# Far queries copied into contiguous tiles by GpSimd, in the attention of a hybrid decoder layer

## The chip, the core and the metric

One core of a Trainium2 chip runs the whole program. Its engines run side by side, each through its own instructions in order: TensorE (PE: matmuls; PEld: the loads of the weights that a matmul holds still while its other operand streams), VectorE (DVE), ScalarE (ACT), GpSimd (POOL) and SyncE (SP), which here only issues DMAs. The metric is the device time of one execution in microseconds, as a median over runs. The profile is of one execution more.

## What is computed

One decoder layer over 2048 positions of width 1024, in float32: an input projection; eight heads of dilated attention beside pooling groups; an output projection; a gated MLP; an embedding gate; a last norm. The change concerns the attention. Cut from the reference:

```python
DIL_PATTERNS = ((128, 1), (512, 4), (2048, 16))
...
    s = jnp.einsum('bnqrhd,bnkrhd->bnrhqk', qb, kk)      # query blocks against [previous, current] keys
    s = s - slopes[:, None, None] * dist                 # ALiBi
    s = jnp.where(valid[:, None, None], s, -jnp.inf)
    m = jnp.max(s, axis=-1, keepdims=True)
    e = jnp.exp(s - m)
    den = jnp.sum(e, axis=-1)
    o = jnp.einsum('bnrhqk,bnkrhd->bnqrhd', e, vv) / den_t[..., None]
...
    w = d * jnp.exp(m - jnp.max(m, axis=0, keepdims=True))
    w = w / jnp.sum(w, axis=0, keepdims=True)
    return jnp.sum(w[..., None] * o, axis=0)             # branches weighted by their denominators
```

Dilation d joins positions of the same residue modulo d. The kernel treats dilation 1 as the near branch and dilations 4 and 16 together as the far branch, by residues modulo 4.

## The kernel before

Attention (`phase_attention`) runs after the input projection and before the output projection and the rest. It has 128 steps: eight heads with sixteen blocks of 128 queries. For the near branch the block is 128 neighbouring positions; for the far branch it is 128 positions of one residue r modulo 4 (every fourth position), against 128, 256, 384 or 512 keys of that residue. Four steps make up a head's residue; it begins with the step of 512 keys, by the order `CFG["perm"]`, and the others have 256, 384 and 128.

A head's queries lie in two tiles, `qhh` and `qll` (high and low parts of the float32 numbers, 128 x 2048), the keys in `ks`, biases in `nb` and `fb`. SP loads them a head ahead. In a step TensorE forms the near scores `sn` (L573, L574: weights are slices of `qhh` and `qll`, keys stream) and the far scores `sf` (L562, L563); VectorE adds the bias and finds the extreme (L578, L584); ScalarE takes the exponential (L590, L594); TensorE transposes (`tp`, L604); ScalarE and VectorE split the result (`pth`, L617; `ptl`, L621); TensorE multiplies by the values (`o`, L632, L646). Before, the far queries were read with a step of four elements:

```python
            t.qr = t.qhh.rearrange("p (c r) -> p r c", r=4)
```

Once a residue, a result `o` of the far and one of the near branch is copied to a staging tile `ev` (by ScalarE and VectorE, L670). Half of it has to change partitions: SP sends it by a DMA (`s<-ev`, L671) into `s1` (near) or `s3` (far), and three steps later GpSimd adds the other half (L672). After each pair of heads the statistics are turned, stored to DRAM (`std`, `stf`) and read back in another layout (`sn`, `sf` of L809, not the scores), and weights `wd` are stored. Later, while the next pair runs, the two branches of the finished pair are mixed in four chunks of 512 positions: SP fetches weights `wb` (L913), GpSimd multiplies `s1` and `s3` by them and adds (`m1`, `m3`, L940, L942, L949), and SP stores the sum to `mr` (L952). For the third pair the chunks come every four steps, for the others every seven. The fourth pair is mixed by VectorE at the start of the output projection, whose weights are `wo` (raw: `rwo`, L985).

The instructions of PE, ACT, DVE and POOL stand in the order in which this code issues them: in each step the stages of `CFG["ord"]`, with their lags. Stage F is the far scores, G the sums on GpSimd, M the mixing. SP's DMAs are placed by the framework. A tile with several buffers can be written again when its last reader is done; a wait for that stands on the engine or queue that writes it.

Of the kernel before, what the change touches and what calls it, by code (L numbers as in the profile page):

```python
# [10 lines left out]
F32 = mybir.dt.float32  # L11
F32R = mybir.dt.float32r
AF = mybir.ActivationFunctionType
ALU = mybir.AluOpType
# [3 lines left out]
P = 128  # L18
# [8 lines left out]
CH = 512  # L27
NCH = S // CH
NQ = S // P
# [21 lines left out]
def fp(ap):  # L51
    return ap.bitcast(F32)


def rdma(nc, dst, src):
    nc.sync.dma_start(fp(dst) if dst.dtype == F32R else dst, fp(src) if src.dtype == F32R else src)
# [429 lines left out]
def phase_attention(tc, g, mx, near_b, far_b):  # L486
# [3 lines left out]
    nc = tc.nc  # L490
    NS = H * NQ
    LAST = 4 * H - 2
    with ExitStack() as ctx:
        sb = ctx.enter_context(tc.tile_pool(name="b_sb", bufs=1, reuse_waits="tile"))
# [5 lines left out]
        heads, steps, groups, pairs = {}, {}, {}, {}  # L500

        def load_qk(h):
            t = heads[h] = Shared()
            pr, e = h // 2, h % 2
            rows = slice(DH * e, DH * e + DH)
            t.qhh = sb.tile([P, S], F32R, tag=f"qhh{e}", bufs=1, name=f"qhh{h}")
            t.qll = sb.tile([P, S], F32R, tag=f"qll{e}", bufs=1, name=f"qll{h}")
            t.qr = t.qhh.rearrange("p (c r) -> p r c", r=4)
            t.qlr = t.qll.rearrange("p (c r) -> p r c", r=4)
            t.ks = sb.tile([P, NCH, 4, P], F32R, tag=f"ks{e}", bufs=1, name=f"ks{h}")  # L510
            t.nb = sb.tile([P, 256], F32, tag=f"nb{e}", bufs=1, name=f"nb{h}")
            t.fb = sb.tile([P, 512], F32, tag=f"fb{e}", bufs=1, name=f"fb{h}")
            twice = lambda z: z[pr][rows, None].to_broadcast([DH, 2, S])
            return [
                (t.qhh, twice(g.qh)),
                (t.ks.rearrange("p c r j -> p (c r j)"), g.kk[pr][rows].rearrange("d a c r j -> d a (c r j)")),
                (t.qll, twice(g.ql)),
                (t.fb, far_b[h]),
                (t.nb, near_b[h]),
            ]  # L520
# [5 lines left out]
        def load_v(pr, which, q):  # L526

            v = sb.tile([P, 4, 2, P], F32R, tag=which, bufs=4, name=f"{which}_{pr}_{q}")
            vals[pr, which, q] = v
            src = near_v[:, 4 * q : 4 * q + 4, pr, :] if which == "v1" else far_v[q, :, :, pr, :]  # L530
            return v.rearrange("p b h d -> p b (h d)"), src
# [24 lines left out]
        def far_scores(s):  # L556
            st = steps[s]
            t = st.t
            st.fv = ps_f.tile([P, CH], F32, tag="f", name="sf")[:, : st.wf]
            keys = t.ks[:, : st.nf, st.r, :]  # L560
            cl = slice(st.i * P, (st.i + 1) * P)
            nc.tensor.matmul(st.fv, t.qr[:, st.r, cl], keys, start=True, stop=False)  # L562
            nc.tensor.matmul(st.fv, t.qlr[:, st.r, cl], keys, start=False, stop=True)  # L563

        def near_scores(s):
            st = steps[s]
# [91 lines left out]
        def halves(pt, gi, near):  # L658
            h, q = divmod(gi, 4)
            e = h % 2  # L660
            mine = slice(DH * e, DH * e + DH)
            other = slice(DH * (1 - e), DH * (1 - e) + DH)
            return e, mine, other, pt.s1[:, q * CH : (q + 1) * CH] if near else pt.s3[:, q, :]

        def copy_out(copy, gi, near):

            e, mine, other, dst = halves(pairs[gi // 8], gi, near)
            o = groups[gi].o[near]
            t = sb.tile([P, CH], F32, tag="ev", bufs=8, name="ev")
            copy(t, o)  # L670
            nc.sync.dma_start(dst[mine], t[other])  # L671
            sums.later(3, lambda: nc.gpsimd.tensor_tensor(dst[mine], dst[mine], t[mine], op=ALU.add))  # L672

        def add_out(gi, near):
            e, mine, other, dst = halves(pairs[gi // 8], gi, near)
            o = groups[gi].o[near]
            ev = sb.tile([P, CH], F32, tag="ev", bufs=8, name="ev")
            nc.scalar.copy(ev[mine], o[other])
            nc.vector.tensor_tensor(dst[mine], o[mine], ev[mine], op=ALU.add)

# [20 lines left out]
        def fold(v):  # L701
            gi, part = v // 4, v % 4
            if part == 1 and gi < LAST:
                copy_out(nc.scalar.copy, gi, False)
# [44 lines left out]
        with tc.manual_schedule(engines=set(EN.values())):  # L749
            for dst, src in load_qk(0):  # L750
                rdma(nc, dst, src)
            for q in range(4):
                for which in ("v3", "v1"):
                    rdma(nc, *load_v(0, which, q))
            queue = []
            stages = {
                "F": far_scores, "N": near_scores, "fm": far_max, "nm": near_max, "fe": far_exp, "ne": near_exp,
                "T": turn, "h": high, "l": low, "V": values, "W": values_b, "S": stats, "M": mix, "o": fold, "p": folded, "B": begin, "G": shifts
            }
            for s in range(NS + 10):  # L760
                if s < NS:
                    h, n = divmod(s, NQ)
                    if n == 1 and h + 1 < H:
                        queue += load_qk(h + 1)
                    if queue and n % 2:
                        rdma(nc, *queue.pop(0))
                    for pr in range(1, NPAIR):
                        if s - 2 * NQ * (pr - 1) in V_STEPS:
                            rdma(nc, *load_v(pr, *V_STEPS[s - 2 * NQ * (pr - 1)]))
                if s == NS + 2:  # L770
                    last_far(nc, g, mx, ps_t, pairs[NPAIR - 1])
                    pieces = pairs[NPAIR - 1].pieces = last_weights(nc, mx, pairs[NPAIR - 1])
                for nm, lag in CFG["ord"]:
                    if 0 <= s - lag < NS or nm in "MG":
                        stages[nm](s - lag)
                for _ in range({NS + 3: 3, NS + 4: 2, NS + 5: 1}.get(s, 0)):
                    next(pieces)
# [63 lines left out]
def last_weights(nc, sb, pt):  # L841

    both = (pt.near, pt.far)
    lo = sb.tile([P, CH], F32, tag="m1", bufs=2, name="lo")[:8]
    nc.vector.tensor_tensor(lo, pt.near[0], pt.far[0], op=ALU.min)
    yield
    for mx_, _ in both:
        nc.vector.tensor_tensor(mx_, lo, mx_, op=ALU.subtract)
    yield
    for ex, _ in both:  # L850
        nc.scalar.activation(ex, ex, AF.Exp)
    yield
    for ex, dn in both:
        nc.vector.tensor_tensor(dn, ex, dn, op=ALU.mult)
    yield
    nc.vector.tensor_tensor(lo, pt.near[1], pt.far[1], op=ALU.add)
    yield
    nc.vector.reciprocal(lo, lo)
    yield
    pt.w = []  # L860
    for ex, _ in both:
        hi, low = (sb.tile([P, CH], F32R, tag=f"wb{y}", bufs=2, name=f"w{y}")[:8] for y in range(2))
        nc.vector.tensor_tensor(ex, ex, lo, op=ALU.mult)
        nc.scalar.copy(hi, ex)
        nc.vector.tensor_tensor(low, ex, fp(hi), op=ALU.subtract)
        pt.w.append((hi, low))
    yield
# [47 lines left out]
    pt.__dict__.setdefault("wb", {})[c] = wb  # L915


def mix_products(nc, g, sb, eng, pt, c):
    cs = slice(c * CH, (c + 1) * CH)
    wb = pt.wb.pop(c)  # L920
    m1 = sb.tile([P, CH], F32, tag="m1", bufs=2, name="m1")
    m3 = sb.tile([P, CH], F32, tag="m3", bufs=1, name="m3")
    eng.tensor_tensor(m1, pt.s1[:, cs], wb[0], op=ALU.mult)
    eng.tensor_tensor(
        m3.rearrange("p (i r) -> p i r", r=4),
        pt.s3.rearrange("p r i -> p i r")[:, c * P : c * P + P, :],
        wb[1].rearrange("p (i r) -> p i r", r=4),
        op=ALU.mult,
    )
    eng.tensor_tensor(m1, m1, m3, op=ALU.add)  # L930
    pt.m1 = m1


def mix_steps(nc, g, sb, pr, pt, c):

    cs = slice(c * CH, (c + 1) * CH)
    wb = pt.wb.pop(c)
    m1 = sb.tile([P, CH], F32, tag="m1", bufs=2, name="m1")
    m3 = sb.tile([P, CH], F32, tag="m3", bufs=1, name="m3")
    nc.gpsimd.tensor_tensor(m1, pt.s1[:, cs], wb[0], op=ALU.mult)  # L940
    yield
    nc.gpsimd.tensor_tensor(  # L942
        m3.rearrange("p (i r) -> p i r", r=4),
        pt.s3.rearrange("p r i -> p i r")[:, c * P : c * P + P, :],
        wb[1].rearrange("p (i r) -> p i r", r=4),
        op=ALU.mult,
    )
    yield
    nc.gpsimd.tensor_tensor(m1, m1, m3, op=ALU.add)  # L949
    yield  # L950
    yield
    nc.sync.dma_start(g.mr[pr][:, cs], m1)  # L952
    yield


# [1054 lines left out]
```

## Time and profile before

| | us |
|---|---|
| median of 3 runs | 2401.07 (2400.24 to 2404.44) |
| the profiled execution | 2395.55 |
| its span, first to last instruction | 2393.7 |
| attention: first near score to last far score | 398 to 655 |
| mean granted TensorE clock | 0.986 |

In the rows of the profile, `out<-in` names the tile that is written and those that are read, the shape is partitions x elements, `x128` a count, and what stands behind `|` is busy time and the mean duration of one in ns, then the idle time of the engine just before them and what ended it. In a timeline a row has its start, its duration, engine and line; a `q` behind an engine's name means its queue, as for DMA issues. The chain that ended last is followed back from the last instruction, at each step to what released it; its pieces are time on that path.

### The profile page before, as it was taken

Reading aid. Unit: us, or ns where it says so; the run is one execution under the profiler, and the core shown is the slowest. Engines: PE = TensorE matmul, PEld = TensorE weight load, DVE = VectorE, ACT = ScalarE, POOL = GpSimd, SP = SyncE. Lnnn points to the kernel's source line nnn. Section 1 sums busy time; section 2 is a strip of 40 time slices with the busy share of each in tenths; the row PEclk is TensorE's granted clock in tenths of the full one; section 3 lists DMA queues with packets and bytes.
Section 4 is the critical chain, followed back from the end, with each engine's and each line's share of the span. In section 5 each row is a group of like instructions: output and inputs, shape, how many; then the busy total and the mean of one; then the engine's idle time right before and its main releaser. Section 6 shows DMA issues by size and latency. Waiting matters only on the chain.

```text
span 2393.7 us, 32711 instructions
## 1 busy us (share of the span) xinstructions
PE 2317.8 (97%) x11251; PEld 1961.5 (82%) x11251; DVE 1711.8 (72%) x2684; ACT 1123.8 (47%) x2040; POOL 567.2 (24%) x540
## 2 busy tenths in 40 slices
PE   8999999999979999999999999999999999999998
PEld 7888888998858878888887877888878888888888
DVE  6644445888863678999999999777766565755665
ACT  5433324998822244454546444544444444444332
POOL 3322122355520133333430666000020000001000
PEclk9999999999989999999999999999999999999999
DMA  7534436777476664556567777444497776654332
GB/s 239 177 136 171 168 132 257 268 250 246 137 238 207 224 212 152 183 191 208 188 216 237 270 262 272 158 145 147 140 322 247 241 243 205 224 170 156 119 102 93
DMA packets 241318, 475.99 MB, mean 199 GB/s; under 512 B 37472, under 2 KB 63904, under 8 KB 238080
## 3 DMA queue, kind: packets, MB, share of 16 engines
q1 hardware_dynamic: 206768, 397.79, 49.8%
q0 software_dynamic: 14736, 48.34, 5.7%
q10 hardware_dynamic: 19648, 27.77, 3.3%
q8 instruction: 88, 1.44, 0.2%
q14 instruction: 78, 0.64, 0.1%
HBM read 309.14 MB, written 156.79 MB: 195 GB/s over the span
## 4 chain that ended last, share of the span: by engine, by line
PE 80%; DVE 7%; DMA 4%; issue 3%; ACT 1%; POOL 0%; ACTq 0%; DVEq 0%; POOLq 0%; SPq 0%
PE ua L1357 16%; PE uc L1357 8%; PE dn L90 6%; PE dn L91 6%; PE dn L89 6%; PE ub L1357 4%; PE z L91 4%; PE z L89 4%; PE z L90 4%; PE tp L604 2%; PE o L91 2%; PE o L89 2%; PE o L90 2%; PE gp L89 2%; PE gp L91 2%
## 5 line engine op out<-in xcount | busy, mean ns | idle before, releaser
L90 PE MATMUL dn<-al,wu 128*128 128x512 f32 x616 | 240.2, 390 | 4.3 <-DVE al L85 4.2
L89 PE MATMUL dn<-ah,wu 128*128 128x512 f32 x616 | 240.0, 390 | 0.0
L91 PE MATMUL dn<-ah,wu 128*128 128x512 f32 x616 | 239.8, 389 | 0.0
L85 DVE TENSOR_TENSOR al<-ra,ah 128x512 fp32r<-128x512 f32 x154 | 105.6, 688 | 111.7 <-ACT ah L84 108.4
L89 PE MATMUL z<-hnh,wh 128*128 128x512 f32 (+1 forms) x480 | 170.2, 355 | 9.6 <-ACT hnh L252 6.1
L90 PE MATMUL z<-hnl,wh 128*128 128x512 f32 (+1 forms) x480 | 169.9, 354 | 3.1 <-DVE hnl L253 2.9
L91 PE MATMUL z<-hnh,wl 128*128 128x512 f32 (+1 forms) x480 | 169.7, 353 | 2.3 <-POOL wl L85 1.7
L84 ACT CAST ah<-ra 128x512 fp32r<-128x512 f32 x154 | 95.2, 621 | 146.0 <-PE dn L91 131.6
L90 PEld LDWEIGHTS dn<-al,wu 128*128 128x128 f32 x616 | 115.7, 188 | 30.0 <-DVE al L85 6.0
L85 DVE TENSOR_TENSOR wu<-ru,wu 128x1024 fp32r<-128x1024 f32 x88 | 135.0, 1534 | 3.9 <-ACT wu L84 3.9
L89 PEld LDWEIGHTS dn<-ah,wu 128*128 128x128 f32 x616 | 115.7, 188 | 24.0
L91 PEld LDWEIGHTS dn<-ah,wu 128*128 128x128 f32 x616 | 115.7, 188 | 23.9
L1357 PE MATMUL ua<-s1h,wu 128*128 128x512 f32 x352 | 116.9, 393 | 3.8 <-ACT ug L1584 3.8
L1357 PE MATMUL uc<-a22h,wu 128*128 128x512 f32 x352 | 115.8, 390 | 4.0 <-DVE uv L1380 4.0
L1357 PE MATMUL ua<-s2h,wu 128*128 128x512 f32 x352 | 116.0, 391 | 1.5 <-ACT ug L1558 1.3
L1357 PE MATMUL ua<-s4h,wu 128*128 128x512 f32 x352 | 116.7, 393 | 0.4 <-ACT uv L1605 0.4
L1357 PE MATMUL ua<-a11h,wu 128*128 128x512 f32 x352 | 115.8, 390 | 0.0
L1357 PE MATMUL uc<-s3h,wu 128*128 128x512 f32 x352 | 115.6, 389 | 0.0
L1357 PE MATMUL ub<-a12h,wu 128*128 128x512 f32 x352 | 115.5, 389 | 0.0
L155 DVE TENSOR_TENSOR acc<-acc,sq 128x512 f32<-128x512 f32 (+1 forms) x125 | 83.8, 670 | 44.0 <-ACT sq L154 30.7
L85 DVE TENSOR_TENSOR wu<-rw,wu 128x512 fp32r<-128x512 f32 x149 | 100.8, 685 | 19.6 <-ACT wu L84 19.4
L89 PEld LDWEIGHTS z<-hnh,wh 128*128 128x128 f32 x480 | 94.0, 196 | 21.6 <-ACT hnh L252 6.1
(334 smaller groups left out, 6651.3 us busy)
## 6 DMA issues: line engine op xcount, KB each, us to landing
ru<-in_w_up_dram SPq DMA_DIRECT2D x66, 512.0 KB, 4.1
wr<-in_w_in_dram SPq DMA_DIRECT2D x64, 256.0 KB, 4.1
rw<-in_w_down_dram SPq DMA_DIRECT2D x61, 256.0 KB, 3.8
nt<-h SPq DMA_DIRECT2D x56, 256.0 KB, 3.9
td<-t SPq DMA_DIRECT2D x22, 512.0 KB, 2.6
t<-td SPq DMA_DIRECT2D x22, 512.0 KB, 3.8
nt<-in_w_down_dram POOLq DMA_DIRECT2D x44, 256.0 KB, 5.0
ra<-oq0s SPq DMA_DIRECT2D x44, 256.0 KB, 3.7
```

Of the source, the lines that this page charges most:

```text
L84: nc.scalar.copy(hi, src)
L85: (low or nc.gpsimd).tensor_tensor(lo, src, fp(hi), op=ALU.subtract)
L89: nc.tensor.matmul(ps, wh, ah, start=first, stop=False, skip_group_check=again)
L90: nc.tensor.matmul(ps, wh, al, start=False, stop=False, skip_group_check=again)
L91: nc.tensor.matmul(ps, wl, ah, start=False, stop=last, skip_group_check=again)
L155: nc.vector.tensor_tensor(acc[:, :n], acc[:, :n], sq[:, :n], op=ALU.add)
L604: nc.tensor.transpose(st.tp[:, bs], st.ee[:, bs], g.ident)
L1357: nc.tensor.matmul(pst, x[:, ksl], y, start=first and k == 0 and n == 0, stop=k == HK - 1 and n == 2, skip_group_check=True)
```

## The change

GpSimd copies the far queries of a residue (one pair of copies, from `qhh` and `qll`) into contiguous tiles `qf` of 128 x 512, three steps before the residue's first far score; those tiles give the far scores' weights. `qf` has four buffers, two pairs. The staging tile `ev` has six buffers where it had eight, `m1` one where it had two. The mixed sum goes into the slice of `s1` that it was made from, and leaves from there.

```diff
-            t.qr = t.qhh.rearrange("p (c r) -> p r c", r=4)
-            t.qlr = t.qll.rearrange("p (c r) -> p r c", r=4)
+            t.by_r = [z.rearrange("p (c r) -> p r c", r=4) for z in (t.qhh, t.qll)]
+            t.qf = {}
...
-            nc.tensor.matmul(st.fv, t.qr[:, st.r, cl], keys, start=True, stop=False)
-            nc.tensor.matmul(st.fv, t.qlr[:, st.r, cl], keys, start=False, stop=True)
+            for x, q in enumerate(t.qf[st.r]):
+                nc.tensor.matmul(st.fv, q[:, cl], keys, start=x == 0, stop=x == 1)
+
+        def gather(s):
+            if s % 4 == 0 and s < NS:
+                h, n = divmod(s, NQ)
+                t = heads[h]
+                t.qf[n // 4] = [sb.tile([P, CH], F32R, tag="qf", bufs=4, name="qf") for _ in range(2)]
+                for dst, src in zip(t.qf[n // 4], t.by_r):
+                    nc.gpsimd.tensor_copy(dst, src[:, n // 4])
...
-            t = sb.tile([P, CH], F32, tag="ev", bufs=8, name="ev")
+            t = sb.tile([P, CH], F32, tag="ev", bufs=6, name="ev")
...
+            gather(0)
             for s in range(NS + 10):
+                gather(s + 3)
...
+def mix_parts(sb, pt, c):
+
+    wb = pt.wb.pop(c)
+    m1 = sb.tile([P, CH], F32, tag="m1", bufs=1, name="m1")
+    m3 = sb.tile([P, CH], F32, tag="m3", bufs=1, name="m3")
+    pt.m1 = near = pt.s1[:, c * CH : (c + 1) * CH]
+    far = pt.s3.rearrange("p r i -> p i r")[:, c * P : c * P + P, :]
+    quads = lambda t: t.rearrange("p (i r) -> p i r", r=4)
+    yield m1, near, wb[0], ALU.mult
+    yield quads(m3), far, quads(wb[1]), ALU.mult
+    yield near, m1, m3, ALU.add
...
 def mix_steps(nc, g, sb, pr, pt, c):
 
-    nc.gpsimd.tensor_tensor(m1, pt.s1[:, cs], wb[0], op=ALU.mult)
+    for out, x, y, op in mix_parts(sb, pt, c):
+        nc.gpsimd.tensor_tensor(out, x, y, op=op)
+        yield
     yield
-    nc.sync.dma_start(g.mr[pr][:, cs], m1)
+    nc.sync.dma_start(g.mr[pr][:, c * CH : c * CH + CH], pt.m1)
     yield
```

First place: TensorE at the first steps of attention, before (the second operand behind the arrow gives the weights).

```order
L573 MATMUL sn_4003<-ks0_3973,qhh0_3971 128x256
L574 MATMUL sn_4003<-ks0_3973,qll0_3972 128x256
L562 MATMUL sf_4006<-ks0_3973,qhh0_3971 128x512
L563 MATMUL sf_4006<-ks0_3973,qll0_3972 128x512
L573 MATMUL sn_4003<-ks0_3973,qhh0_3971 128x256
L574 MATMUL sn_4003<-ks0_3973,qll0_3972 128x256
L562 MATMUL sf_4023<-ks0_3973,qhh0_3971 128x256
L563 MATMUL sf_4023<-ks0_3973,qll0_3972 128x256
```

The same place now.

```order
L581 MATMUL sn_4007<-ks0_3973,qhh0_3971 128x256
L582 MATMUL sn_4007<-ks0_3973,qll0_3972 128x256
L563 MATMUL sf_4010<-ks0_3973,qf_3997 128x512
L563 MATMUL sf_4010<-ks0_3973,qf_3998 128x512
L581 MATMUL sn_4007<-ks0_3973,qhh0_3971 128x256
L582 MATMUL sn_4007<-ks0_3973,qll0_3972 128x256
L563 MATMUL sf_4031<-ks0_3973,qf_3997 128x256
L563 MATMUL sf_4031<-ks0_3973,qf_3998 128x256
```

Nothing moves on TensorE; the far scores take their weights from `qf`, a pair of which serves four steps.

Second place: GpSimd from the last DMA issue of the phase before on, in the first heads, before.

```order
L464 DMA ml7_114<-ml_3931 128x512
L672 TENSOR_TENSOR s3_4000<-s3_4000,ev_4195 64x512
L672 TENSOR_TENSOR s1_3999<-s1_3999,ev_4224 64x512
L672 TENSOR_TENSOR s3_4000<-s3_4000,ev_4299 64x512
L672 TENSOR_TENSOR s1_3999<-s1_3999,ev_4328 64x512
```

GpSimd there now.

```order
L464 DMA ml7_114<-ml_3931 128x512
L571 COPY qf_3997<-qhh0_3971 128x512
L571 COPY qf_3998<-qll0_3972 128x512
L571 COPY qf_4017<-qhh0_3971 128x512
L571 COPY qf_4018<-qll0_3972 128x512
L571 COPY qf_4101<-qhh0_3971 128x512
L571 COPY qf_4102<-qll0_3972 128x512
L571 COPY qf_4197<-qhh0_3971 128x512
L571 COPY qf_4198<-qll0_3972 128x512
L680 TENSOR_TENSOR s3_4004<-s3_4004,ev_4211 64x512
L571 COPY qf_4305<-qhh1_4021 128x512
L571 COPY qf_4306<-qll1_4022 128x512
```

The four pairs of head 0 stand ahead of the first sum, the first pair of head 1 (step 16) right behind it, and so on: each later pair stands between a sum of the far branch and the sum of the near branch that follows it.

Third place: SP's queue in the last residues, where the third pair of heads is mixed (`mr2`), before.

```order
L952 DMA mr2_97<-m1_7222 128x512
L671 DMA s3_6674<-ev_7202 64x512
L913 DMA wb1_7283<-wd2_125 64x512
L671 DMA s1_6673<-ev_7235 64x512
L913 DMA wb1_7283<-wd2_125 64x512
L913 DMA wb0_7395<-wd2_125 64x512 x2
L952 DMA mr2_97<-m1_7337 128x512
L671 DMA s3_6674<-ev_7317 64x512
L913 DMA wb1_7398<-wd2_125 64x512 x2
L671 DMA s1_6673<-ev_7350 64x512
L952 DMA mr2_97<-m1_7451 128x512
```

SP's queue there now.

```order
L952 DMA mr2_97<-s1_5796 128x512
L679 DMA s3_6774<-ev_7322 64x512
L923 DMA wb1_7403<-wd2_125 64x512 x2
L679 DMA s1_6773<-ev_7355 64x512
L923 DMA wb0_7519<-wd2_125 64x512 x2
L679 DMA s3_6774<-ev_7441 64x512
L952 DMA mr2_97<-s1_5796 128x512
L923 DMA wb1_7522<-wd2_125 64x512
L679 DMA s1_6773<-ev_7474 64x512
L923 DMA wb1_7522<-wd2_125 64x512
L952 DMA mr2_97<-s1_5796 128x512
```

The second of the three stores to `mr2` stood ahead of the shift of the next far result (`s3<-ev`) and stands behind it now; the first and the third stand as before.

More of the change, by code (lines that the diff above doesn't have):

```diff
@@ L676, in add_out @@
             o = groups[gi].o[near]
-            ev = sb.tile([P, CH], F32, tag="ev", bufs=8, name="ev")
+            ev = sb.tile([P, CH], F32, tag="ev", bufs=6, name="ev")
             nc.scalar.copy(ev[mine], o[other])
@@ L843, in last_weights @@
     both = (pt.near, pt.far)
-    lo = sb.tile([P, CH], F32, tag="m1", bufs=2, name="lo")[:8]
+    lo = sb.tile([P, CH], F32, tag="m1", bufs=1, name="lo")[:8]
     nc.vector.tensor_tensor(lo, pt.near[0], pt.far[0], op=ALU.min)
@@ L915, in mix_fetch @@
     pt.__dict__.setdefault("wb", {})[c] = wb
-def mix_products(nc, g, sb, eng, pt, c):
[L919 to L931, printed above, removed]
-def mix_steps(nc, g, sb, pr, pt, c):
[L936 to L940, printed above, removed]
-    yield
[L942 to L952, printed above, removed]
+def mix_parts(sb, pt, c):
[8 more added lines that the diff above has]
+    yield near, m1, m3, ALU.add
+def mix_products(nc, g, sb, eng, pt, c):
+    for out, x, y, op in mix_parts(sb, pt, c):
+        eng.tensor_tensor(out, x, y, op=op)
+def mix_steps(nc, g, sb, pr, pt, c):
+    for out, x, y, op in mix_parts(sb, pt, c):
+        nc.gpsimd.tensor_tensor(out, x, y, op=op)
+        yield
+    yield
+    nc.sync.dma_start(g.mr[pr][:, c * CH : c * CH + CH], pt.m1)
     yield
```

## The prediction

> **What bounds the kernel now.** I read the engines' shares and a table of stretches first, then the groups by line and form inside attention, then the chain that ended last, then the queues of GpSimd (POOL) and SyncE (SP) in order of time.
>
> ```profile
> PE 2317.8 (97%) x11251; PEld 1961.5 (82%) x11251; DVE 1711.8 (72%) x2684; ACT 1123.8 (47%) x2040; POOL 567.2 (24%) x540
> 444.00:454.00 10.00, 10.00 (x73) 9.83 (x72) 9.00 (x30) 9.74 (x32) 2.56 (x2) 1.00 0.53 161
> ```
>
> The second row is a stretch inside attention (398 to 657 us), in the order PE, PEld, DVE, ACT, POOL, clock, DMA share. TensorE never idles there, but VectorE is at 9.0 and ScalarE at 9.74 of 10. The change touches attention alone, so the whole run's 47% for ScalarE says nothing: a faster TensorE meets ScalarE at once. POOL looks free there; it is not everywhere, as the last fence shows.
>
> The groups of weight loads in 398 to 657 us (busy, mean ns):
>
> ```profile
> L563 PEld LDWEIGHTS sf<-ks,qll 128*128 128x128 f32 x128 | 42.3, 330 | 0.0
> L562 PEld LDWEIGHTS sf<-ks,qhh 128*128 128x128 f32 x128 | 39.8, 311 | 0.0
> L574 PEld LDWEIGHTS sn<-ks,qll 128*128 128x128 f32 x128 | 25.6, 200 | 0.0
> L573 PEld LDWEIGHTS sn<-ks,qhh 128*128 128x128 f32 x128 | 25.1, 196 | 10.4 <-DVE st L578 10.3
> ```
>
> Same tiles, same shape, same count. The near scores read 128 neighbouring columns (196 and 200 ns), the far scores every fourth column (311 and 330 ns). The stride is the only difference: 115 to 130 ns a load.
>
> **What a load is worth on the path.** Busy time of loads overlaps the matmuls, so I price it from the chain, whose pieces are time on the path (start, us, what):
>
> ```profile
> 641.59 0.12 PE sn L573
> 641.71 0.12 PE sn L574
> 641.83 0.35 PE sf L562
> 642.18 0.23 PE sf L563
> 643.45 0.23 PE sf L562
> 645.25 0.29 PE sf L562
> 647.26 0.17 PE sf L562
> 705.15 0.23 PE o L90
> ```
>
> The four L562 pieces are the steps with 512, 256, 384 and 128 keys; L563 takes 0.23 in each. A pair costs 0.58, 0.46, 0.52 and 0.40. With neighbouring columns a matmul of 256 keys takes 0.12 (L573) and one of 512 takes 0.23 (the row at 705.15, 128x512); between them I take 0.17 for 384, and 0.12 for 128, since a load of 128 columns still has to pass. Pairs then cost 0.46, 0.24, 0.34 and 0.24. Saved: 0.12 + 0.22 + 0.18 + 0.16 = 0.68 us in the four steps of a residue, or 128/4 x 0.68 = 21.8 us at most.
>
> The Trainium skill (TensorE: Matmul & The Clock Gate, Part 2, step 1) says that the next weights load while the current matmul runs, at about 107 ns for 128 columns. By that rule a 512-key matmul would hide the longer load behind it, and the 0.12 of that step would not be there to save (0.56 a residue); the trace disagrees, with 0.35 at 641.83 against 0.23 at 705.15.
>
> **What ScalarE leaves of it.** The timeline shows two 512-key far scores, with which a residue starts, and two rows of ScalarE between them:
>
> ```profile
> 428.17 0.52 PE L562 MATMUL sf<-ks,qhh 128*128 128x512 f32 x1
> 430.41 0.46 ACT L617 CAST pth<-tp 128x384 fp32r<-128x384 f32 x1
> 430.77 0.58 ACT L670 COPY ev<-o 128x512 f32<-128x512 f32 x1
> 435.52 0.51 PE L562 MATMUL sf<-ks,qhh 128*128 128x512 f32 x1
> ```
>
> A residue takes 7.35 us (428.17 to 435.52). If ScalarE's busy share in the stretch above were a hard floor, only 2.6% of that, 0.19 us, could go. But its rows overlap: the cast of 0.46 is followed after 0.36. By starts to starts of this kind, wherever nothing is waited for, the 21 instructions of a residue add up to about 6.75 us (an estimate from the timeline of 429 to 437 us). So the gain lies between 0.19 and 0.60 a residue by ScalarE and 0.68 by TensorE; the three engines hand work round in a ring of two-deep buffers, so the floor is not reached. I take 0.45.
>
> **How many residues get it.** Of 32, those count whose start follows 7.2 to 7.4 us after the last. The first four are set by loads (below). After each pair of heads the statistics go to DRAM and back, and the engines wait:
>
> ```profile
> 460.64 6.27 DMA std<-sx
> 529.25 12.06 DMA sf<-stf
> ```
>
> Such a latency starts when the pair ends and eats what the steps behind it save, some three residues after steps 32, 64 and 96. The last four fall to POOL (below). That leaves steps 16 to 32, 44 to 64 and 76 to 96: 4 + 5 + 5 = 14 residues x 0.45 = **6.3 us gained**.
>
> **What the copies cost on POOL.** No row copies 128x512 there. The nearest:
>
> ```profile
> L672 POOL TENSOR_TENSOR s<-s,ev 64x512 f32<-64x512 f32 x60 | 76.7, 1286 | 136.9 <-DMA s<-ev 100.7 <-PE sn L573 27.5 <-DVE ev L670 4.2
> L942 POOL TENSOR_TENSOR m<-s,wb 128x512 f32<-128x512 f32 x12 | 18.6, 1553 | 0.2
> L940 POOL TENSOR_TENSOR m<-s,wb 128x512 f32<-128x512 f32 x12 | 15.4, 1281 | 0.4
> L422 POOL COPY tail<-u 128x15 f32<-128x15 f32 x16 | 5.3, 333 | 13.6 <-ACT u L420 12.9
> L152 POOL TENSOR_TENSOR sq<-x 128x256 f32<-128x256 f32 x4 | 3.0, 770 | 0.0
> ```
>
> Ends: 0.33 us (a copy with next to no data) and 1.55 (two inputs, one of them strided). From 256 to 512 elements two inputs cost 0.51 more, 2.0 ns an element, so one input 1.0; a strided input adds 1.55 - 1.28 = 0.27. So 0.33 + 0.51 + 0.27 = 1.1 us, 2.2 for a pair, 32 x 2.2 = 70 us of POOL in a stage of 260. It is nearer the upper end, since the size and a strided read are those of L942. POOL then has 2 x 1.29 (sums) + 2.2 = 4.8 us per residue, and where mixing runs at its slow spacing 2.4 more (1.28, 1.55 and an add like the first, every seven steps): 7.2 of 7.3. That just fits, and lag of a few us is covered: the copies are issued three steps ahead (5.5 us).
>
> The Trainium skill (GPSIMD Engine Reference, section 7) gives 2.9 cycles an element for reads with steps over 8 bytes against 1.9 else, half as much again; the trace shows 21% more (L942 against L940). By the Trainium skill's figure the copy would be an estimated 1.24 us without its fixed part.
>
> **Where POOL is waited for: the start.** POOL runs in order, and the first copies stand behind its last DMA issue of the phase before. The rows, and the issues with the median time to landing:
>
> ```profile
> 400.19 0.56 POOL L464 DMA_DIRECT2D ml<-ml  x1
> 414.27 0.42 SPq L56 DMA_DIRECT2D nb<-in_near_b_dram  x1
> nb<-in_near_b_dram SPq DMA_DIRECT2D x1, 128.0 KB, 13.3
> 428.23 5.03 POOL L672 TENSOR_TENSOR s<-s,ev 64x512 f32<-64x512 f32 x4 [27.49 <-PE sn L573]
> ```
>
> The first pair ends near 400.75 + 2.2 = 403.0 and holds the first far score back by a few us. I count nothing for it, because the next place is fixed by loads. Head 1's bias nb lands at 414.27 + 13.3 = 427.6, and step 16 begins at 428 whatever TensorE saved before. The first sum s<-ev waits behind those loads to 428.23. The copies of step 16 are queued behind that sum: 428.23 + 1.28 + 2.2 = 431.7, where the far score ran at 428.17. **3.5 us lost.** What is queued behind the waiting matmul is all of TensorE, and ScalarE and VectorE run dry; the next residue's copies (at 436) are in time again.
>
> **The end.** In the last four residues mixing runs twice as close, and POOL and SP already go round in a circle:
>
> ```profile
> 632.86 0.33 SPq L952 DMA_DIRECT2D mr<-m  x1
> 642.90 0.33 SPq L952 DMA_DIRECT2D mr<-m  x1
> 645.63 1.28 POOL L672 TENSOR_TENSOR s<-s,ev 64x512 f32<-64x512 f32 x1 [2.76 <-DMA s<-ev]
> 648.78 0.52 PE L562 MATMUL sf<-ks,qhh 128*128 128x512 f32 x1
> 655.31 0.33 SPq L952 DMA_DIRECT2D mr<-m  x1
> 658.08 2.49 POOL L672 TENSOR_TENSOR s<-s,ev 64x512 f32<-64x512 f32 x2 [2.80 <-DMA s<-ev]
> 664.78 0.33 SPq L952 DMA_DIRECT2D mr<-m  x1
> 666.40 1.03 SPq L985 DMA_DIRECT2D rwo<-in_w_out_dram  x2
> ```
>
> SP holds the shift s<-ev until POOL has mixed the chunk for mr, and POOL waits 2.8 us for the shift: 9.5 us a turn (655.31 to 664.78), longer than a residue, and at its end SP issues the first weights of the output projection. Three pairs of copies enter those turns: +6.6 us. Against that, SP now has the second mr behind the next shift (the third place shown with the change), so that this shift travels beside the mixing. Worked through with 2.2 to land, 1.3 a sum, 2.2 a pair and 4.2 the mixing: first mr 632.86 + 2.2 = 635.1; shift issued 635.5, landed 637.8, then 1.3 + 2.2 + 1.3 + 4.2: second mr 646.8. Its shift left at 645.1, landed 647.3, plus the same 9.0: third mr 656.3. The last turn has no copies: landed 658.9, plus 1.3 + 1.3 + 4.2: fourth mr 665.7, and after two shifts rwo at 667.4, **1.0 us later** than before. The last residue's copies end at 650.8, 2.0 past 648.78; TensorE waits there, but the phase behind starts from rwo.
>
> **Costed at nothing.** Mixing in place has the same three instructions; m1 with one buffer is written and read by one engine in order. mr leaves from s1, which is written again 64 steps later. Six ev tiles: a tile is wanted again 9 steps (16 us) after its sum is issued; if POOL lagged that far, ScalarE's copy would stall.
>
> **Sum.** -6.3 + 3.5 + 1.0 = -1.8 us. The profiled execution took 2395.55, 1.85 over its span; the median is 2401.07, 0.23% above it. From the median: **2399 us**, within 0.2%, which is about what a measurement of this kernel can tell from no change.
>
> **Rivals.** Faster: POOL's copy is cheap, 0.65 us, about halfway from the empty copy to my value, and ScalarE lets 0.6 a residue through. Then 14 x 0.6 = 8.4, less 2.6 at step 16; the end gains 6 x 0.45 - 1.0 = 1.7: -7.5, so 2393.6. For it: half of L940's time is its second input. Against: the stride.
>
> Slower: POOL becomes the bound. At 1.5 us a copy, L942's price, slow mixing needs 2.6 + 2.4 + 3.0 = 8.0 us a residue, over the 7.35; the eight mixing residues of the 14 gain nothing (6 x 0.45 = 2.7), step 16 loses 4.3, and the end 1.0 + 6 x 0.4 = 3.4: +5.0, so 2406. It decides from about 1.3 us a copy. For it: L942. Against: a copy has one input. The Trainium skill's 2.9 cycles (GPSIMD Engine Reference, section 7), with a fixed part of 0.33 added, would make this the case that comes: an estimated 1.57 us a copy.
>
> No effect: the load's length does not set the pace, nothing is saved: +4.5, 2405.6. Against it: the chain's 0.17 to 0.35 on L562.
>
> **Chances.** Forecast 0.42; cheap copies 0.32; POOL the bound 0.22; no effect 0.04. So faster 0.32, same 0.42, slower 0.26. The range takes in cheap copies with all of TensorE's 0.68 (14 x 0.68 - 2.6 + 1.7 = 8.6) and a little for the residues that I gave nothing, and the slow case with 3 us of lag at other residues: 2390 to 2409. The forecast's own range is 2396 to 2403.
>
> **What will show it.** Loads of the far scores at about 200 ns instead of 311 and 330; copies at 1.1 us; residues at 6.9 us in 436 to 457 and around 500; a gap on TensorE of some 3 us near 428 that POOL ends; rwo within 3 us of 666. The forecast is wrong if copies cost under 0.8 or over 1.3, if residues stay at 7.3, or if POOL's lag reaches TensorE in the middle.

## The result, and the profile after

The changed kernel takes 2417.38 us (median of 5 runs, 2411.93 to 2420.45), the kernel before 2400.85 beside it: a ratio of 1.0059, with an interval of 1.004 to 1.0078. A second measurement of the two gave 1.0038 (1.002 to 1.0057). So it is slower, by 0.4 to 0.6%. The forecast was 2399 in a range up to 2409, and slower had a chance of 0.26.

The groups of copies after, in 398 to 665 us (busy, mean ns, idle before), and the weight loads of the far scores, by form:

```profile
L571 POOL CAST qf<-qhh 128x512 fp32r<-128x512 f32 x32 | 35.6, 1114 | 8.8 <-PE sf L563 8.2
L571 POOL CAST qf<-qll 128x512 fp32r<-128x512 f32 x32 | 35.6, 1113 | 0.0
```

```profile
L563 PEld LDWEIGHTS sf<-ks,qf 128*128 128x128 f32 x255 | 42.6, 200 | 23.1 <-POOL qf L571 23.1
```

The copy costs 1.11 us and the load 200 ns instead of 311 and 330, both as priced. Where nothing waits, a residue has become shorter, as the starts of three in the timeline show:

```profile
437.69 0.63 PE L563 MATMUL sf<-ks,qf 128*128 128x512 f32 x2
444.43 0.62 PE L563 MATMUL sf<-ks,qf 128*128 128x512 f32 x2
451.15 0.63 PE L563 MATMUL sf<-ks,qf 128*128 128x512 f32 x2
```

That is 6.74 and 6.72 us, where the same residues took 7.22 and 7.11. So the gain is there, and something eats more than all of it. The waits of 398 to 676 us (engine, line, releaser: us in total, times, longest):

```profile
PEld sf L563 <- POOL qf L571: 23.1, 19, 3.9
PE sf L563 <- POOL qf L571: 18.0, 19, 3.7
POOL s L680 <- DMA s<-ev: 52.1, 21, 10.0
```

TensorE now waits 18 us for copies, and GpSimd itself still waits 52 us for shifts. Before (398 to 657 us) that last row was:

```profile
POOL s L672 <- DMA s<-ev: 95.1, 29, 9.0
```

Half of TensorE's wait lies in the last head. At its first residue (step 112) TensorE had lost nothing against before, in these rows of before and after:

```profile
627.10 0.52 PE L562 MATMUL sf<-ks,qhh 128*128 128x512 f32 x1
626.99 0.50 PE L563 MATMUL sf<-ks,qf 128*128 128x512 f32 x1 [0.79 <-POOL qf L571]
```

At its last it was 8.7 us late (648.78 before). In the second executions of the two kernels the same holds, counted from the first near score: 0.4 us late at step 112, 8.0 at step 124. Here are the two latest waits of after, and the chain that ended last at the same place:

```profile
647.16 0.50 PE L563 MATMUL sf<-ks,qf 128*128 128x512 f32 x1 [3.66 <-POOL qf L571]
657.43 0.50 PE L563 MATMUL sf<-ks,qf 128*128 128x512 f32 x1 [1.06 <-POOL qf L571]
```

```profile
651.81 3.13 DMA s<-ev
655.07 1.27 POOL s L680
656.34 2.08 POOL qf L571 x2
658.47 0.80 PE sf L563
```

The chain reads: a shift, its sum, the copies behind that sum, the far score. Through the copies TensorE has become a link in the circle of SP and GpSimd. SP's rows at the end (start, duration):

```profile
642.10 0.33 SPq L952 DMA_DIRECT2D mr<-s  x1
653.52 0.33 SPq L952 DMA_DIRECT2D mr<-s  x1
663.78 0.33 SPq L952 DMA_DIRECT2D mr<-s  x1
673.22 0.33 SPq L952 DMA_DIRECT2D mr<-s  x1
674.84 1.02 SPq L985 DMA_DIRECT2D rwo<-in_w_out_dram  x2
```

rwo leaves 8.4 us later than the 666.40 of before. But the four stores span 31.1 us, against 31.9 before: the turns are no slower. It is the first that is 9.2 us late, and its cause stands further ahead. GpSimd's timeline of before, from the last mixing of the second pair to the third store `wd` (weights for the third pair):

```profile
608.22 1.28 POOL L672 TENSOR_TENSOR s<-s,ev 64x512 f32<-64x512 f32 x1 [5.62 <-DMA s<-ev]
609.57 1.29 POOL L940 TENSOR_TENSOR m<-s,wb 128x512 f32<-128x512 f32 x1
...
613.89 1.27 POOL L949 TENSOR_TENSOR m<-m,m 128x512 f32<-128x512 f32 x1
616.57 0.80 POOL L901 DMA_DIRECT2D wd<-wts  x1 [1.41 <-DVE wts L900]
```

The same place after:

```profile
608.79 1.28 POOL L680 TENSOR_TENSOR s<-s,ev 64x512 f32<-64x512 f32 x1
614.57 1.27 POOL L680 TENSOR_TENSOR s<-s,ev 64x512 f32<-64x512 f32 x1 [4.50 <-ACT ee L598]
615.92 1.28 POOL L949 TENSOR_TENSOR m<-s,wb 128x512 f32<-128x512 f32 x1
617.15 1.09 POOL L571 CAST qf<-qhh 128x512 fp32r<-128x512 f32 x1
618.18 1.08 POOL L571 CAST qf<-qll 128x512 fp32r<-128x512 f32 x1
...
622.35 1.29 POOL L949 TENSOR_TENSOR s<-m,m 128x512 f32<-128x512 f32 x1
623.59 0.80 POOL L911 DMA_DIRECT2D wd<-wts  x1
```

Before, GpSimd was done first and waited 1.41 us for the weights; after, the weights wait for GpSimd, and `wd` leaves 7.0 us later. (The releaser named at 614.57 had long been done. The chain of after names a shift, whose landing fits.)

```profile
605.54 8.89 DMA s<-ev
614.58 1.27 POOL s L680
```

This shift was issued at 605.54, right behind the store of a mixed chunk at 605.11, and then travelled 8.89 us among the loads of the next head. Before, that store had left at 599.83 and the shift at 603.95, and the sum ran at 608.22, so the shift took 4.3 us at most. Of the 6.4 us by which the sum is late, 1.6 thus lie in the shift's issue and the greater part in its travel: in the 10 us from 605 the DMA engines moved 342 GB/s, before 181 (in the second executions 322 and 191). So the circle of GpSimd and SP runs at the slow spacing too, and all twelve stores to `mr` are 4 to 11 us late, from the first (509.2, before 504.3) on.

From the first near score to the last store to `mr`, attention with the head of the output projection took 305.1 us before and 316.3 after, in second executions 307.2 and 315.1. From there to the end it was 1690.5 and 1697.2, in the second 1693.2 and 1688.7. So the 8 to 11 us belong to attention; the 6.7 that the first two profiles show behind it are chance, and runs differ by as much. The granted TensorE clock of 398 to 716 us was 0.93 in both executions of the changed kernel and 0.94 in both of before. How much of the loss came through the clock is not separated here.

### The profile page after: what moved, and what is told of

Read it like the earlier page. It is cut to its first block, busy times and chain, and to the rows that moved or that the text cites. A ratio compares the mean times of both kernels' runs of the same rounds, so it can differ in the third digit from the quotient of the medians.

```text
span 2411.6 us, 32807 instructions
## 1 busy us (share of the span) xinstructions
PE 2311.5 (96%) x11251; PEld 1942.6 (81%) x11251; DVE 1709.5 (71%) x2684; ACT 1120.5 (46%) x2040; POOL 633.6 (26%) x604
## 4 chain that ended last, share of the span: by engine, by line
PE 72%; DVE 10%; DMA 5%; issue 4%; ACT 4%; POOL 2%; SPq 0%; ACTq 0%; POOLq 0%; DVEq 0%
PE ua L1357 15%; PE uc L1357 7%; PE dn L90 6%; PE dn L91 6%; PE dn L89 6%; PE ub L1357 4%; PE z L91 4%; PE z L89 4%; PE z L90 4%; PE o L91 2%; PE gp L89 2%; PE o L89 2%; PE gp L91 2%; PE gp L90 2%; PE o L90 2%
```

## The experiments

Three theories. **One**: place in the queue. GpSimd works in order, and a copy behind a sum inherits the wait for that sum's shift. **Two**: GpSimd's added work, 71 us, wherever it stands. **Three**: the side changes. The table gives all kernels; "attention" is the stretch just named, from one profiled execution.

| kernel | ratio to before (95%) | attention, us |
|---|---|---|
| before, again | 0.9996 (0.9984 to 1.0008) | 307.2 |
| the changed kernel | 1.0059 (1.004 to 1.0078) | 316.3 |
| the changed kernel, again | 1.0038 (1.002 to 1.0057) | 315.1 |
| e3: side changes alone | 1.0005 (0.9992 to 1.0018) | 302.9 |
| e4: short loads, no copies | 0.9977 (0.9962 to 0.9991) | 305.6 |
| e2: copies made, not used | 1.0045 (1.0029 to 1.0061) | 311.5 |
| e8: as e2, four steps ahead | 1.0012 (0.9996 to 1.0028) | 305.3 |
| e1: copies four steps ahead | 1.0004 (0.999 to 1.0018) | 308.9 |
| e5: no copies in the last head | 1.0029 (1.0017 to 1.0042) | 309.0 |
| e6: e1 and e5 together | 1.0004 (0.9991 to 1.0017) | 302.9 |
| e7: e1, mr from GpSimd's queue | 1.0027 (1.0011 to 1.0043) | 310.6 |
| x1: wd from ScalarE's queue | 1.0045 (1.0029 to 1.0061) | 314.1 |
| x4: before, wd likewise | 1.0001 (0.9989 to 1.0014) | 305.5 |
| x2: e1 and x1 | 0.9992 (0.9981 to 1.0003) | 301.3 |
| x3: e6 and x1 | 0.9986 (0.9972 to 0.9999) | 298.8 |
| x5: x3, two waits fewer | 0.9975 (0.9962 to 0.9988) | 296.9 |

**The parts alone.** Side changes without copies (e3), and short loads without copies (e4, which leaves out the selection of the residue's queries and multiplies others):

```diff
             for x, q in enumerate(t.qf[st.r]):
-                nc.tensor.matmul(st.fv, q[:, cl], keys, start=x == 0, stop=x == 1)
+            # e3: t.by_r, q[:, st.r, cl]      e4: (t.qhh, t.qll), q[:, st.n * P : st.n * P + P]
-                gather(s + 3)
```

> No copies, strided weights as before; what is left of the change is mixing in place, one m1, six staging tiles and the order of SP's queue that follows from them. Theories 1 and 2: within 0.1% of before, 2399 to 2403, rwo between 664 and 667. Theory 3: 2408 or more, rwo after 670.

> No copies; the far scores read neighbouring columns of the query tiles, which leaves out the selection of a residue's queries (other queries are multiplied). It prices the shorter loads by themselves. By the prediction 14 residues gain 0.45 us each: 6.3 us, so 2394 to 2396, with residues of 6.7 to 6.9 us. If ScalarE or the statistics eat it up: 2399 to 2402 with the same short residues. If all 32 residues carry it: 2385 to 2388.

e3 made no difference that can be measured: theory three falls. e4 gained 5 us (median 2395.1 against 2400.17; the interval says 2 to 9), near the 6.3 of the prediction. Its profiled execution took 2399.41, and attention there is no shorter than before (305.6 us), so no trace shows where the 5 us arise. It does show where the rest of TensorE's gain stops, in rows of TensorE, SP and VectorE:

```profile
639.68 0.39 PE L563 MATMUL sf<-ks,qhh 128*128 128x512 f32 x1
668.26 1.03 SPq L983 DMA_DIRECT2D rwo<-in_w_out_dram  x2
666.66 0.68 DVE L853 TENSOR_TENSOR lo<-nr,fr 8x512 f32<-8x512 f32 x1 [6.13 <-POOL s L947]
```

The last residue begins 9.1 us earlier than before (648.78), though attention began 1.0 later, and rwo leaves 1.9 later. GpSimd and SP hold it back. The third row is a cost that I had put at nothing: `lo`, VectorE's first tile of the last weights, uses the tag `m1`, which has one buffer now, and waits 6.1 us for GpSimd's last add to finish reading it.

**Copies that nobody reads.** GpSimd makes all copies; the far scores read strided queries.

> GpSimd makes all copies as in the changed kernel, but the far scores read the strided queries as before, so TensorE never waits for a copy and gains nothing by shorter loads. Theory 1 (TensorE's waits are most of the loss): the last residue begins within 1.5 us of the 648.8 of before; what is left is SP's late rwo, up to 6 us, so 2402 to 2408. Theory 2 (GpSimd's work alone delays shifts, mixing and rwo): rwo at 673 to 676 as in the changed kernel, and 2409 to 2416. Theory 3 (side changes): 2409 to 2416 too, but then e3_side shows the same.

TensorE never waits for a copy here, and still 11 us are lost: rwo left at 678.54, 7.0 later than before when both are counted from the first near score. TensorE's waits for copies are thus not needed for a loss of this size, against theory one; the lag travels through shifts, mixing and rwo, as theory two had it. (e2 lacks the gain of the short loads too.) In e2 it also reaches TensorE by another way, the statistics, in which all engines wait for a few small operations of VectorE. One of them before and in e2 (min, median, max ns), and what TensorE waited for in e2:

```profile
L895 DVE TENSOR_TENSOR dn<-wts,sn x3: 179/181/653, 478.5 to 615.1; 128x32 f32<-128x32 f32 x3
```

```profile
L905 DVE TENSOR_TENSOR dn<-wts,sn x3: 198/980/1172, 485.5 to 622.3; 128x32 f32<-128x32 f32 x3
```

```profile
PE sn L581 <- DVE st L586: 14.9, 6, 4.0
```

The 24 operations of the statistics take 12.2 and 12.1 us in the two executions of before, 16.6 in e2, 13.0 in e8 and 6.8 in e4; TensorE's wait of the last row was 8.5 and 10.2 before. In the two executions of the changed kernel itself they take only 11.7 and 8.8, and TensorE waits 7.1 and 3.9, so there this way costs no more than before. Why they stretch is shown at the end.

**The place in the queue.** One number: copies one step earlier, which puts them ahead of the far sum instead of behind it.

```diff
-                gather(s + 3)
+                gather(s + 4)
```

> One number changes: a residue's copies are issued four steps ahead instead of three, which puts them ahead of the far sum in GpSimd's order instead of behind it; GpSimd does the same work. Theory 1 (the place in the queue: a copy behind a sum hands the wait for that sum's shift on to TensorE): TensorE's waits for copies (18.0 us, and 23.1 on its weight loads) fall below 8 in all, the turns at the end go back from 10 to 11 us to about 9.5, since the copies then run while GpSimd waits for the shift, rwo is issued near 667 to 670 instead of 674.8, and the time is 2399 to 2408. Theory 2 (GpSimd's work: 71 us more on it, wherever it stands): waits and turns stay, 2414 to 2419. Theory 3 (side changes: the order of SP's queue, six staging tiles, mixing in place): no change, 2415 to 2419.

> Copies four steps ahead, but the far scores read the strided queries. It asks what GpSimd's copies cost besides TensorE's waits when they stand ahead of the sums. If place in the queue is all of it: within 4 us of before, 2399 to 2404, where e2_unused with three steps took 11 more. If the work itself costs (VectorE's small operations of the statistics last 1.2 us instead of 0.2 while GpSimd works, and sums and shifts lag): 2406 to 2412. Were parts to add up, e1_lead4 (+1) less e4_ceiling (-5) gives +6: 2406.

The loss goes: e1 1.0004 instead of 1.0059, and e8 1.0012 instead of e2's 1.0045. The work is the same to the copy, so theory two falls as a sum of work: it is the place. A copy ahead of the sum runs while GpSimd waits for the shift anyway. The copies are still not free there: e1 has the short loads and none of the 5 us that e4 gained by them. The waits in e1:

```profile
PE sf L563 <- POOL qf L571: 9.5, 9, 3.3
POOL qf L571 <- PE sf L563: 27.3, 11, 4.2
POOL s L680 <- DMA s<-ev: 37.3, 21, 5.2
```

TensorE's wait for copies is halved (I had expected under 8), and 3.3 of the 9.5 are the first far score. GpSimd now waits 27 us for free `qf` buffers (the second row): it is ahead of TensorE instead of behind. Turns were not 9.5 throughout, as I had expected, but 10.6, 9.4 and 9.5.

**The end.** No copies in the last head, with three steps (e5) and four (e6); and the stores to `mr` from GpSimd's queue (e7).

```diff
-            if s % 4 == 0 and s < NS:
+            if s % 4 == 0 and s < NS - NQ:      # e5, e6; strided weights there
...
-    nc.sync.dma_start(g.mr[pr][:, c * CH : c * CH + CH], pt.m1)
+    nc.gpsimd.dma_start(g.mr[pr][:, c * CH : c * CH + CH], pt.m1)      # e7
```

> The changed kernel with copies three steps ahead, but none in the last head, whose four residues read the strided queries. It takes the copies out of the circle of GpSimd and SP at the end and leaves the others. If the end carries the loss (rwo 8.4 us late, of which some 6 arise in the last four residues): rwo at 668 to 671 and 2406 to 2411. If the loss arises in the heads before (waits for copies at 401, 522, 618, lags of the sums, collisions of VectorE's small statistics operations with GpSimd): 2412 to 2417.

> Copies four steps ahead, and none in the last head. If the last head's copies are what still costs with four steps (its last residue waits 3 us, the first turn at the end is 10.6 instead of 9.5): rwo 2 to 3 us earlier than the 668.2 of e1_lead4 and 2396 to 2400, faster than before by up to 0.2%. If rwo is set by GpSimd's and SP's chain from 604 us on, in which no copy of the last head stands until step 108: rwo within 1.5 us of 668.2 and 2399 to 2403.

> Copies four steps ahead in all heads; the stores to mr leave from GpSimd's queue right behind the add instead of from SP's, so SP no longer holds a shift back until GpSimd has mixed a chunk. If the circle of the two queues sets the end: turns fall to GpSimd's own work of 8 to 9 us (two sums 2.6, copies 2.2, mixing 4.1 less than all of it in a turn at 4 steps), rwo at 663 to 666, TensorE's wait in the last residue under 1 us, 2395 to 2400. If GpSimd's work is the bound there: turns as in e1_lead4, 2400 to 2405.

e5 lies between (2406.7), but its interval overlaps that of the changed kernel's second measurement, so the last head's share is not settled. Its rwo leaves at 674.35, 273.0 from the first near score (after 276.8, before 268.2), and its third `wd` 225.1 from there (after 225.5, before 218.4): with no copies at the end most of the lag at `wd` and half of that at rwo is still there, so it is older. e6 adds nothing measurable to e1. e7 was a miss: rwo did leave earlier, at 664.76, but the time rose by 5 us against e1, and the last residue began at 657.16. SP's blocked store was not the whole circle. Each store now takes GpSimd's time ahead of copies and sums, and the granted clock of 398 to 716 us was 0.91 (e1: 0.94); which of the two is why was not followed up.

**The store wd.** By now the suspect was the row at 623.59 above. x1 moves that store to ScalarE's queue, one step later, in the changed kernel; x2 does it with four steps, x3 also without copies in the last head; x4 is the control, the kernel before with that alone.

```diff
-    nc.gpsimd.dma_start(
+def mix_weights_store(nc, g, pr, pt):      # called where d == CFG["m"][1] + 1
+    nc.scalar.dma_start(
         g.wd[pr]...
```

> The changed kernel (copies three steps ahead) with one DMA moved: the mixing weights' store wd, three in all, leaves from ScalarE's queue one step after they are computed, instead of from GpSimd's, where the third left 10 us after its weights were ready because GpSimd was behind with sums, copies and mixing. SP's order shifts a little with it. If that store is what hands GpSimd's lag on to the mixing of the third pair and to rwo: third wd 7 to 10 us earlier, first mr of the third pair 4 to 8 us earlier, rwo at 667 to 671 and 2405 to 2411. If GpSimd's lag itself is the bound (mixing stands in its order behind the same work): rwo within 2 us of 674.8 and 2414 to 2419.

> The kernel before, with wd from ScalarE's queue and nothing else: the control for the three others. In the trace of before the third wd left 0.3 us after its weights were ready, so by the theory nothing is to be had: 2399 to 2403. If it is faster by 4 us or more, a gain of the others isn't the copies'.

> Copies four steps ahead, wd from ScalarE's queue. If wd's place hands the rest of the lag on: first mr of the third pair 3 to 5 us earlier than in e1_lead4 and 2395 to 2399, faster than before. If GpSimd's work binds: 2399 to 2403.

> The candidate to beat both: copies four steps ahead, none in the last head, wd from ScalarE's queue. If the shorter loads' gain (5 us by e4_ceiling) is lost only through GpSimd's lag at wd: 2391 to 2396. If not: 2398 to 2402.

In x1 the third `wd` left 11.2 us earlier from the first near score (214.3, after 225.5), yet the first store of the third pair only 3.3 earlier (240.7, after 244.0) and rwo 2.6 (274.2, after 276.8). The median fell from 2417 to 2409, but a repeat of the changed kernel gave 2410, so x1 shows no sure gain. Behind an early `wd` GpSimd's own lag remains: `wd` passes it on but is not alone. Once the copies stand well, it pays: x2 and x3 are 2.1 and 3.3 us below before, x3 just clear of it (at most 0.9999). The control shows none of that gain, so it takes the copies to have it. But SP's order shifts a little with this edit, so in x1 to x3 the store isn't the only thing that moved: TensorE's wait for the statistics (`PE sn <- DVE st`), 9.4 us in e1 and 7.7 in e6, is 1.4 in x2 and 1.5 in x3 (11.1 in the control). How much of the gain is the store's own is not shown.

**Two waits fewer.** x3 with the strided queries in the very first residue, and `lo` in a slot of tag `wb0` instead of `m1`.

```diff
-            if s % 4 == 0 and s < NS - NQ:
+            if s % 4 == 0 and 0 < s < NS - NQ:
...
-    lo = sb.tile([P, CH], F32, tag="m1", bufs=1, name="lo")[:8]
+    lo = sb.tile([P, CH], F32, tag="wb0", bufs=2, name="lo")[:8]
```

> x3 with two more waits taken away: residue 0 reads the strided queries (no copy ahead of the first far score), and VectorE's first tile of the last weights has a slot of its own kind (wb0) instead of the single m1 that GpSimd's last add still reads. If both waits are on the path: 2 to 4 us better than x3, 2392 to 2395. If the loads near 428 and the output weights set the pace there: as x3, 2395 to 2398.

> The changed kernel again, for a second profiled execution. If the loss in the code behind is chance: attention is again 10 to 13 us longer than before, and the rest of the program within 3 us of the kernel before in its own second execution. If the change lengthens the rest: 6 us or more again. 2413 to 2419 in either case.

> The kernel before again, for a second profiled execution: 2398 to 2402. If the first one was a lucky execution of the rest of the program, the rest takes 2 to 5 us longer here than the 1690.5 from the last store of the mixed sum to the end.

x5 beats both kernels: 2393.8 against 2399.93, 0.9975 (0.9962 to 0.9988). Its step beyond x3 (0.9986) lies within the intervals, so what these two waits were worth is not shown. Its last stores to `mr` and its rwo:

```profile
637.23 0.33 SPq L958 DMA_DIRECT2D mr<-s  x1
648.33 0.33 SPq L958 DMA_DIRECT2D mr<-s  x1
657.86 0.33 SPq L958 DMA_DIRECT2D mr<-s  x1
659.47 1.02 SPq L991 DMA_DIRECT2D rwo<-in_w_out_dram  x2
```

rwo leaves 6.9 us earlier than before. Of the two repeats, the kernel before needed 2.7 us more for the untouched rest than in its first execution, and the changed one 8.5 less: the loss there was chance. The changed kernel's median was 2409.66 in its repeat, under the 2413 to 2419 that I had expected.

## Why the prediction was wrong, step by step

- **What a load is worth: right in size.** 200 ns, 0.4 to 0.5 us a residue (0.45 taken), and 5 us in all by e4 (6.3). That the total came so near is partly luck: the sum gave the gain to 14 residues, while e4's TensorE stood 10 us ahead at the last residue, counted from the first near score, and rwo left no earlier for it. By the Trainium skill's rule that the next weights load while the current matmul runs (TensorE: Matmul & The Clock Gate, Part 2, step 1), 0.56 a residue would have been saved instead of 0.68; the residues, 0.4 to 0.5 shorter, can't tell the two apart. The chain can: a pair at 512 keys takes 0.46 to 0.48 us after (0.46 at 451.32, 0.48 at 458.14) and took 0.58 before, so the trace disagrees with the rule.
- **The price of a copy: right**, 1.11 against 1.1. The Trainium skill's factor for strided reads (GPSIMD Engine Reference, section 7) had given an estimated 1.57 us with a fixed part and 1.24 without; the trace is below both.
- **Step 16, 3.5 lost: wrong place, little harm.** TensorE waited 3.3 at the very first far score, which I had counted as hidden by the loads, and 0.55 at step 16. By step 40 the changed kernel stands 0.2 us behind before: the short residues have paid for both.
- **The middle, costed at nothing: the step that failed.** "That just fits, and lag of a few us is covered" added up GpSimd's busy time, 7.2 us in a residue of 7.3. Two things are wrong in it. Residues were to shrink to 6.9 by the same forecast, so it didn't fit. And busy time isn't the measure of an engine that works in order and waits for shifts: 95 us of waiting before, and a copy behind a waiting sum can't use it. e1 shows it, with the same work in another place: 1.0004 instead of 1.0059. The condition for the slower rival (1.5 us a copy, deciding from 1.3) was wrong for the same two reasons. By its own sum, 2.6 + 2.4 and two copies reach a residue of 7.35 at 1.18 us a copy and one of 6.9 at 0.95, and the slower case came at 1.11.
- **The end, +1.0: its starting point failed, its mechanism held.** Turns were forecast at 11.7, 9.5 and 9.4 and came at 11.4, 10.3 and 9.4; SP's new order did pay for three pairs of copies. But "first mr 632.86 + 2.2 = 635.1" took only the copies of that turn; it came at 642.10, 7 us more. The `wd` ahead of it had left 7.0 late, but x1 shows that an early `wd` alone gives back only 3.3 of that; the rest is GpSimd's own lag. The last stretch of the sum inherits the middle's lag. So rwo came 8.4 late, not 1.0.
- **Costed at nothing.** Mixing in place and six staging tiles: right as far as e3 tells. One buffer for `m1` "written and read by one engine in order": wrong, since `lo` shares the tag, though it costs nothing until attention ends earlier (e4, 6.1 us of wait).
- **Sum.** Gains 6.3 and 3.5 lost were about right as sizes. What is missing is 7 us at the end, and on TensorE the gain of the middle. At step 108 e4 stands 8.1 us ahead of before, the changed kernel 1.4, each counted from the first near score; behind step 64 it had even been 4 us late, with copy waits of 1.4 and 0.5 us at that step on top of the statistics. Such readings from one execution are rough: steps 100 to 104 took 11.1 us before, 10.1 in its second execution and 6.8 after.

Open stays how the loss divides between TensorE's waits and the late rwo: e2, without those waits and without the short loads' gain, lost 11, about as much as the changed kernel's two measurements (16.5 and 9.7).

## What to carry to other kernels

A queue that works in order has no slack to give just because it is idle: ask what it is waiting for at that moment, and whether the new work stands ahead of that wait or behind it. One step in the issue order was worth 0.3 to 0.6% here, more than the 0.2% that the copies were made for. And follow a lag to the DMAs that the late engine issues: a store that it sends late starts the next pair's work late.

## What the hardware showed that was not expected

VectorE's tiny operations with two inputs in SBUF (128x32) take about 0.18 us, or up to as long as what GpSimd does beside them. Two timelines of e2, VectorE's and GpSimd's, at the statistics of the second pair:

```profile
551.96 1.17 DVE L905 TENSOR_TENSOR dn<-wts,sn 128x32 f32<-128x32 f32 x1
553.05 1.14 DVE L906 TENSOR_TENSOR dn<-wts,sf 128x32 f32<-128x32 f32 x1
554.22 1.30 DVE L907 TENSOR_TENSOR dn<-dn 128x32 f32<-128x32 f32 x1
```

```profile
551.94 1.13 POOL L571 CAST qf<-qhh 128x512 fp32r<-128x512 f32 x1
553.02 1.11 POOL L571 CAST qf<-qll 128x512 fp32r<-128x512 f32 x1
554.22 1.26 POOL L680 TENSOR_TENSOR s<-s,ev 64x512 f32<-64x512 f32 x1
```

Each of these three starts with an instruction of GpSimd and ends with it, and then meets the next one. In the seventeen profiled executions here there are 357 such operations in the statistics (128x32 and 128x64). 190 of them started while GpSimd was idle, and none took over 0.4 us; of the 167 that started while it worked, 104 did. The Trainium skill (SBUF — State Buffer, Who interferes with whom) says that a VectorE instruction with two SBUF inputs and a GpSimd instruction that reads SBUF contend; the trace agrees, with 1.14 to 1.30 us for 0.18. So work on GpSimd can lengthen VectorE's small operations; in e2, where they stretched most, TensorE also waited longest for the statistics.

A shift of half a tile, 2.2 us in the quiet rows at the end, took 8.89 us at 605.54, while the loads of the next head were under way. And the same code behind attention took 1688.7 to 1697.2 us between executions: a difference of 8 us there proves nothing.
